# Two-layer encoder with three attention forms: the reciprocal roots of the projections' norms and the scale of the scores on GpSimd, lambda computed early in the stage

## Chip, cores and metric

The kernel runs on one core of a Trainium2 chip. The time is that of the whole program on the device, in microseconds (us); smaller is better. A profiled execution shows, for each engine, which instruction ran when: TensorE (PE, and PEld for its weight loads), VectorE (DVE), ScalarE (ACT), GpSimd (POOL) and SyncE (SP, which issues most DMAs).

## The reference, cut to what matters

Two layers over a sequence of 1024 tokens of 1024 features. Each layer normalises its input, projects it with one matrix, whose columns belong to three token mixers, and runs the mixers' attention; an output projection and a feed-forward part follow.

```
xn = _rms_norm(x, attn_norm[l])
h = xn @ w_in[l]
(h_cq, h_ckv, h_kr, h_dq, h_dk, h_dv, h_gq, h_gk, h_gv) = jnp.split(h, IN_OFFSETS, axis=-1)
c_q = _rms_norm(h_cq, mla_q_norm[l])
q_a = (c_q @ mla_w_uq[l]).reshape(B, S, MLA_HEADS, MLA_QK)...
c_kv = _rms_norm(h_ckv, mla_kv_norm[l])
kv_a = (c_kv @ mla_w_ukv[l])...
q_a, k_a = _rms_norm(q_a, mla_q_gain[l]), _rms_norm(k_a, mla_k_gain[l])    # then rotary
q_b = _apply_rope(_rms_norm(q_b, diff_q_gain[l]), cos_dif, sin_dif)
k_b = _apply_rope(_rms_norm(k_b, diff_k_gain[l]), cos_dif, sin_dif)
lam = exp(sum(diff_lq1[l] * diff_lk1[l])) - exp(sum(diff_lq2[l] * diff_lk2[l])) + lambda_init
a = p[:, :, 0] - lam * p[:, :, 1]                                          # differential attention
q_c = axial_rope(_rms_norm(q_c, gqa_q_gain[l]))
k_c = axial_rope(_rms_norm(k_c, gqa_k_gain[l]))
```

`_rms_norm(x, gain)` is x times the reciprocal root of the mean of its squares, times a gain. The softmax scale (width to the power -1/2) is folded into the norm of the queries.

## The kernel before, in words

**Stages of a layer.** The input's norm and the first projection; the other projections; attention (the three mixers' heads one behind the other); output projection and feed-forward. The projections run over groups of output columns: `down` for the two latents (`cq`, `ckv`), `diff_heads` for differential queries and keys in two groups each (`C_DQ`, `C_DK`), `mla_q` and `mla_kv` in two groups of three heads, `gqa_q`, `gqa_rest`, and the values (`diff_v`). Each runs over 8 tiles of 128 tokens. A product in full precision is three matmuls (L159, L160, L161) of high and low parts; the low part of a weight (`wl`, L125) is made on GpSimd here.

**From a tile's product to stored features.** ScalarE copies the sum from PSUM (`raw`), VectorE makes the two rotary products (L344, L349), GpSimd adds them into `half` (L411, L505; L497 multiplies by the gain where there is no rotation), ScalarE squares and VectorE sums the squares into `ssq` (L413, L509). `half` holds four tiles, 512 tokens; there are three such buffers. At each fourth tile `finish` (or the end of `down`) makes the reciprocal roots of all four: `rsq` forms `v` from `ssq` (L149), `newton` a first guess by integer operations (L132, L133) and three rounds of Newton's iteration, for 12 or 16 columns at once (4 in `down`). Then GpSimd multiplies `half` by the roots (L388), and `out_features` is put into the list `later`: TensorE transposes the four tiles (L364, into `pt`), ScalarE makes the high part (`sth`, L368), VectorE the low part (`stl`, L369; L373 with a gain), and SP stores both. In one layer's projections 22 norms go this way; two more, those of the input (`x_norm`), use `rsq` too.

**The rounds.** `newton` has two branches. Without an engine given, a round is three operations on VectorE (L136, L137, L138). With one it is four on that engine (L140 to L143). The norms of the attention's output pass `po` (GpSimd) already, in before too; the projections pass none.

**Lambda.** `neg_lambda` loads four vectors, multiplies two pairs of them on VectorE (L179), sums each product by a matmul with ones (L181, into `pl_`), takes the exponentials on ScalarE (L183) and combines them (L185, L186). In before its call stands at the end of the projections, behind the loop that empties `later`.

**What sets the order.** The context is opened with a scheduler that simulates a timeline (`schedule_with_timeline_sim=True`): each engine's queue is in the order that this simulation found, not in that of the code. Every engine then works through its queue in order and waits where an operand or a buffer isn't ready.

Of the kernel before, what the change touches and what calls it, by code (L numbers as in the profile page):

```python
# [16 lines left out]
ALU = mybir.AluOpType  # L17
# [48 lines left out]
def encoder(ctx: ExitStack, tc: tile.TileContext, a: dict, out: bass.AP):  # L66
    nc = tc.nc
    ve, ac, po, pe, sy = nc.vector, nc.scalar, nc.gpsimd, nc.tensor, nc.sync
# [29 lines left out]
    def ps_u(name):  # L98
        return banks["pool"].tile([P, 512], F32, tag="u", name=name)
# [11 lines left out]
    def f(t):  # L111
        return t.bitcast(F32)
# [14 lines left out]
    def newton(pool, v, n, tag, eng=None):  # L127

        i = pool.tile([P, n], I32, tag=tag + "i", name="i")
        t = pool.tile([P, n], F32, tag=tag + "t", name="t")  # L130
        r = pool.tile([P, n], F32, tag=tag + "r", name="r")
        ve.tensor_scalar(i, v.bitcast(I32), 1, None, ALU.arith_shift_right)  # L132
        ve.tensor_scalar(r.bitcast(I32), i, -1, 0x5F3759DF, ALU.mult, ALU.add)  # L133
        for _ in range(3):
            if eng is None:
                ve.scalar_tensor_tensor(out=t, in0=r, scalar=-0.5, in1=r, op0=ALU.mult, op1=ALU.mult)  # L136
                ve.tensor_tensor(out=t, in0=t, in1=v, op=ALU.mult)  # L137
                ve.scalar_tensor_tensor(out=r, in0=t, scalar=1.5, in1=r, op0=ALU.add, op1=ALU.mult)  # L138
            else:
                eng.tensor_tensor(out=t, in0=r, in1=r, op=ALU.mult)  # L140
                eng.tensor_tensor(out=t, in0=t, in1=v, op=ALU.mult)
                eng.tensor_scalar(t, t, -0.5, 1.5, ALU.mult, ALU.add)
                eng.tensor_tensor(out=r, in0=t, in1=r, op=ALU.mult)  # L143
        return r

    def rsq(pool, ssq, n, inv, scale, tag):

        v = pool.tile([P, n], F32, tag=tag + "v", name="v")
        ve.tensor_scalar(v, ssq, inv / scale**2, EPS / scale**2, ALU.mult, ALU.add)  # L149
        return newton(pool, v, n, tag)  # L150

    def gain_cols(src, n, name):
        t = lay.tile([P, n], F32, tag=name, name=name)
# [19 lines left out]
    def neg_lambda(l):  # L173
        lam_init = 0.8 - 0.6 * math.exp(-0.3 * l)
        lq = lay.tile([64, 4], F32, tag="lq", name="lq")
        for i, n in enumerate(("diff_lq1", "diff_lq2", "diff_lk1", "diff_lk2")):
            sy.dma_start(out=lq[:, i : i + 1], in_=a[n][l].unsqueeze(1))
        lp = lay.tile([64, 2], F32, tag="lp", name="lp")
        ve.tensor_mul(lp, lq[:, 0:2], lq[:, 2:4])  # L179
        pl_ = ps_u("pl_")  # L180
        pe.matmul(pl_[:, 0:2], ones[:64, :], lp, start=True, stop=True)  # L181
        le = lay.tile([P, 2], F32, tag="le", name="le")
        ac.activation(le, pl_[:, 0:2], AF.Exp)  # L183
        nlam = lay.tile([P, 1], F32, tag="nlam", name="nlam")
        ve.tensor_tensor(out=nlam, in0=le[:, 1:2], in1=le[:, 0:1], op=ALU.subtract)  # L185
        ve.tensor_scalar(nlam, nlam, -lam_init, None, ALU.add)  # L186
        return nlam
# [11 lines left out]
    for l in range(L):  # L199
# [15 lines left out]
        bp = tc.alloc_tile_pool(name=f"b{l}", bufs=2, side=there, reuse_waits="tile")  # L215
# [51 lines left out]
        def r_of(tt):  # L267
            return rx[tt // 4][:, tt % 4 : tt % 4 + 1]
# [24 lines left out]
        def run(*chunks):  # L293

            for _ in zip_longest(*chunks):
                pass
# [57 lines left out]
        def halves(n, nh):  # L354

            t = bp.tile([P, 4 * n], F32, tag="half", name="half", bufs=3, padded_shape=[P, 4 * 384])
            ssq = bp.tile([P, 4 * nh], F32, tag="ssq", name="ssq", bufs=3, padded_shape=[P, 16])
            return t.rearrange("p (t n) -> p t n", n=n), ssq.rearrange("p (t h) -> p t h", h=nh)

        def out_features(g, t, pieces, gains=None):  # L360
            for j, (c0, w, rows) in enumerate(pieces):
                pt = ps_u("pt")
                for i in range(4):
                    pe.transpose(pt[:w, i * P : (i + 1) * P], t[:, i, c0 : c0 + w], ident)  # L364
                h = bp.tile([P, 512], F32R, tag="sth", name="sth")[:w]
                lo = bp.tile([P, 512], F32R, tag="stl", name="stl")[:w]
                if gains is None:
                    ac.copy(h, pt[:w])  # L368
                    ve.tensor_tensor(out=lo, in0=pt[:w], in1=f(h), op=ALU.subtract)  # L369
                else:  # L370
                    gj = gains[:w, j : j + 1]
                    ac.activation(h, pt[:w], AF.Copy, scale=gj)
                    ve.scalar_tensor_tensor(  # L373
                        out=lo, in0=pt[:w], scalar=gj, in1=f(h), op0=ALU.mult, op1=ALU.subtract
                    )
                for part, st in ((0, h), (1, lo)):
                    sy.dma_start(out=rows[part][:, g * 512 : (g + 1) * 512], in_=f(st))

        def finish(g, t, ssq, nh, width, pieces, scaled):

            n = 4 * nh
            whole = width**-0.5 if scaled == nh else 1.0
            r = rsq(bp, ssq.rearrange("p t h -> p (t h)"), n, 1.0 / width, whole, "q")
            if 0 < scaled < nh:
                rv = r.rearrange("p (t h) -> p t h", h=nh)[:, :, :scaled]
                ve.tensor_scalar(rv, rv, float(width**-0.5), None, ALU.mult)
            tv = t.rearrange("p t (h x) -> p (t h) x", x=width)
            po.tensor_tensor(  # L388
                out=tv, in0=tv, in1=r.unsqueeze(2).to_broadcast([P, n, width]), op=ALU.mult
            )  # L390
            later.append([LAG, lambda: out_features(g, t, pieces)])
# [54 lines left out]
        def down(w, n, keep, gains, dst, extra):  # L446
            state = {}

            def emit(tt, ps):
                if tt % 4 == 0:  # L450
                    state["t"], state["ssq"] = halves(keep, 1)
                t, ssq = state["t"], state["ssq"].rearrange("p t h -> p (t h)")
                i = tt % 4
                ve.tensor_scalar_mul(t[:, i, :], ps[:, :keep], r_of(tt))
                if extra:
                    extra(tt, ps)
                ac.activation(work("sq", keep), t[:, i, :], AF.Square, accum_out=ssq[:, i : i + 1])
                if i == 3:
                    r = rsq(bp, ssq, 4, 1.0 / keep, 1.0, "q")
                    for j in range(4):  # L460
                        ve.tensor_scalar_mul(t[:, j, :], t[:, j, :], r[:, j : j + 1])
                    g = tt // 4
                    pieces = [(c0, P, [x[c0 : c0 + P] for x in dst]) for c0 in range(0, keep, P)]
                    later.append([LAG, lambda: out_features(g, t, pieces, gains)])

            return project(xn, KT, w, n, emit)

        def latent(src, nk):

            out = []  # L470
            for part in range(2):
                tiles = []
                for k in range(nk):
                    for th in range(2):
                        t = ops.tile([P, 512], F32R, tag="ab"[part], name="lat")
                        sy.dma_start(
                            out=f(t), in_=src[part, k * P : (k + 1) * P, th * 512 : (th + 1) * 512]
                        )
                        tiles.append(t)
                out.append(lambda k, tt, ts=tiles: ts[2 * k + tt // 4][:, tt % 4 * P : (tt % 4 + 1) * P])  # L480
            return out
# [72 lines left out]
        def diff_heads(col, c, gain, dst, scaled):  # L554
            pieces = [(j * P, P, rows_of(dst, 4 * c + 2 * j, 2)) for j in range(2)]
            t = tabs(gain, T_DIFF, DD, 32)
            return heads64(col + 256 * c, 4, 0, [(0, 4, t)], 32, pieces, 4 if scaled else 0)
# [16 lines left out]
        xpool.release()  # L574
        ops = tc.alloc_tile_pool(name=f"o{l}", bufs=10, side=here, reuse_waits="tile")
        run(diff_heads(C_DQ, 0, gd_q, qd, True))
        lat = latent(cqd, 3)
        tq = tabs(gq_m, T_MLA, ROPE, ROPE // 2)
        run(mla_q(0, tq))
# [12 lines left out]
        run(diff_v(1))  # L592
        for _, e in later:
            e()
        nlam = neg_lambda(l)
        bp.release()
        xnp.release()

# [32 lines left out]
        with tc.tile_pool(name=f"c{l}", bufs=2, side=there, reuse_waits="tile") as cp:  # L631
            QB = 256
            n = QB // P
# [91 lines left out]
            class Single:  # L725


                tag = "b"
# [31 lines left out]
            class Diff:  # L760
                tag = "a"
# [162 lines left out]
            while lagging or spreads or products or ends:  # L924
                done = front()
                whole = done is not False and not (fronts or twice[0])
# [280 lines left out]
        for ft in range(FT):  # L1207
# [3 lines left out]
            if ft % 2:  # L1211
# [3 lines left out]
                t = wr.tile([P, 2048], F32, tag="hs", name="hs", bufs=1)  # L1215
# [30 lines left out]
        for p0 in range(0, NP, NC):  # L1246
            n = min(NC, NP - p0)
# [102 lines left out]
```

## Time and profile before

| | us |
|---|---|
| median of three runs | 3217.32 |
| lowest and highest | 3216.38, 3220.18 |
| the profiled execution's own time | 3216.48 |
| its span in the profile | 3214.7 |

In the profiled execution TensorE is busy for 3080.5 us (96%), its weight loads for 84%, VectorE for 2317.8 us (72%), ScalarE for 1586.4 us (49%) and GpSimd for 1137.4 us (35%). A share over the span mixes stages with different limits, so the trace is read by stages. In layer 0 the projections behind the first one run from 86.6 to 373.4 us, and attention to 839.6; in layer 1 from 1684.2 to 1969.3, and attention to 2437.0. A row of the timeline names when an instruction began, how long it took, its engine, line and operands, and, in brackets, how long its engine had been idle before it and what it waited for.

### The profile page before, as it was taken

Reading aid. Unit: us, or ns where it says so; the run is one execution under the profiler, and the core shown is the slowest. Engines: PE = TensorE matmul, PEld = TensorE weight load, DVE = VectorE, ACT = ScalarE, POOL = GpSimd, SP = SyncE. Lnnn points to the kernel's source line nnn. Section 1 sums busy time; section 2 is a strip of 40 time slices with the busy share of each in tenths; the row PEclk is TensorE's granted clock in tenths of the full one; section 3 lists DMA queues with packets and bytes.
Section 4 is the critical chain, followed back from the end, with each engine's and each line's share of the span. In section 5 each row is a group of like instructions: output and inputs, shape, how many; then the busy total and the mean of one; then the engine's idle time right before and its main releaser. Section 6 shows DMA issues by size and latency. Waiting matters only on the chain.

```text
span 3214.7 us, 49930 instructions
## 1 busy us (share of the span) xinstructions
PE 3080.5 (96%) x17628; PEld 2697.1 (84%) x17628; DVE 2317.8 (72%) x4224; ACT 1586.4 (49%) x3010; POOL 1137.4 (35%) x1562
## 2 busy tenths in 40 slices
PE   8899899999998999989998998999999989999999
PEld 8899888888787888878898997888887878888787
DVE  5987788888347666677679877888882575665776
ACT  5444578877334333333254445878782443333332
POOL 1645477776102100100026454777771110111000
PEclk9999999999999999999999999999999999999999
DMA  5576633435652333473344756433356433335633
GB/s 155 160 215 196 197 114 106 120 101 156 201 187 76 104 112 99 137 248 128 98 157 144 230 181 184 126 101 111 103 154 223 157 95 99 101 106 168 223 123 102
DMA packets 386073, 466.14 MB, mean 145 GB/s; under 512 B 36768, under 2 KB 275360, under 8 KB 385824
## 3 DMA queue, kind: packets, MB, share of 16 engines
q1 hardware_dynamic: 372416, 418.38, 42.2%
q0 software_dynamic: 13408, 44.57, 4.2%
q8 instruction: 140, 2.29, 0.3%
q14 instruction: 109, 0.89, 0.1%
HBM read 313.42 MB, written 149.42 MB: 144 GB/s over the span
## 4 chain that ended last, share of the span: by engine, by line
PE 74%; DVE 12%; DMA 5%; ACT 3%; issue 3%; POOL 1%; SPq 1%; ACTq 0%; DVEq 0%; POOLq 0%
PE sc L681 8%; PE pv L890 8%; PE ptc L704 5%; PE psa L159 5%; PE psa L161 5%; PE psa L160 5%; PE psy L160 4%; PE psy L161 4%; PE psy L159 4%; PE psb L161 3%; PE psb L159 3%; PE psb L160 3%; PE psc L161 2%; PE psc L160 2%; PE psc L159 2%
## 5 line engine op out<-in xcount | busy, mean ns | idle before, releaser
L681 PE MATMUL sc<-k,q 128*128 128x512 f32 (+1 forms) x1472 | 417.7, 412 | 15.9 <-ACT p L689 9.0
L688 DVE TENSOR_REDUCE nm<-sc 128x1 f32<-128x1024 f32 x320 | 389.4, 1217 | 53.6 <-PE sc L681 50.6
L689 ACT ACTIVATE p<-sc,nm 128x1024 f32<-128x1024 f32 x320 | 358.7, 1121 | 66.2 <-DVE nm L688 51.7
L159 PE MATMUL psb<-wh,xl 128*128 128x256 f32 (+2 forms) x1280 | 381.1, 302 | 6.7 <-ACT wh L124 4.8
L160 PE MATMUL psb<-wl,xh 128*128 128x256 f32 (+2 forms) x1280 | 379.4, 298 | 7.7 <-POOL wl L125 7.5
L161 PE MATMUL psb<-wh,xh 128*128 128x256 f32 (+2 forms) x1280 | 377.4, 297 | 0.0
L710 DVE TENSOR_TENSOR pl<-ptc,ph 128x512 fp32r<-128x512 f32 x512 | 337.2, 680 | 34.6 <-ACT ph L709 33.0
L709 ACT CAST ph<-ptc 128x512 fp32r<-128x512 f32 x512 | 286.7, 586 | 75.7 <-PE ptc L704 65.4
L681 PEld LDWEIGHTS sc<-k,q 128*128 128x128 f32 (+1 forms) x1472 | 258.0, 190 | 66.7 <-ACT p L689 20.9
L704 PE MATMUL ptc<-ident,p 128*128 128x128 f32 x2048 | 289.7, 275 | 14.4 <-DVE pl L710 7.5
L890 PE MATMUL pv<-ph,v 128*128 128x256 f32 x1280 | 300.3, 287 | 0.0
L890 PE MATMUL pv<-pl,v 128*128 128x256 f32 x1024 | 277.7, 296 | 8.1 <-DVE ot L756 6.2
L704 PEld LDWEIGHTS ptc<-ident,p 128*128 128x128 f32 x2048 | 240.4, 142 | 47.1 <-POOL p L794 7.7
L1222 POOL DMA_DIRECT2D hd<-h x66 | 36.0, 545 | 680.5 <-DVE h L1163 434.8
L159 PE MATMUL psy<-bh,al 128*128 128x512 f32 x616 | 241.1, 394 | 14.7 <-DVE al L125 14.7
L160 PEld LDWEIGHTS psb<-wl,xh 128*128 128x128 f32 x1280 | 245.5, 192 | 10.6 <-POOL wl L125 10.1
L159 PEld LDWEIGHTS psb<-wh,xl 128*128 128x128 f32 x1280 | 244.9, 192 | 10.4 <-ACT wh L124 6.4
L744 POOL TENSOR_SCALAR p<-p,rec 128x1024 f32<-128x1024 f32 x192 | 215.0, 1123 | 107.5 <-DVE rec L694 84.7
L161 PEld LDWEIGHTS psb<-wh,xh 128*128 128x128 f32 x1280 | 245.1, 192 | 0.0
L160 PE MATMUL psy<-bl,ah 128*128 128x512 f32 x616 | 241.2, 392 | 0.1
L161 PE MATMUL psy<-bh,ah 128*128 128x512 f32 x616 | 240.5, 391 | 0.0
L124 ACT CAST wh<-ws 128x512 fp32r<-128x512 f32 x176 | 108.5, 622 | 266.9 <-PE psa L161 236.0
(222 smaller groups left out, 7654.6 us busy)
## 6 DMA issues: line engine op xcount, KB each, us to landing
graw<-in_w_gate_up SPq DMA_DIRECT2D x88, 512.0 KB, 5.5
ar<-hd SPq DMA_DIRECT2D x28, 1024.0 KB, 6.1
hd<-hs POOLq DMA_DIRECT2D x88, 256.0 KB, 3.1
hd<-h POOLq DMA_DIRECT2D x66, 256.0 KB, 2.4
q<-qd SPq DMA_DIRECT2D x256, 64.0 KB, 2.4
B<-od SPq DMA_DIRECT2D x12, 1280.0 KB, 6.8
wraw<-in_w_in SPq DMA_DIRECT2D x56, 256.0 KB, 3.5
o<-od SPq DMA_DIRECT2D x10, 1280.0 KB, 11.5
```

Of the source, the lines that this page charges most:

```text
L124: (hi_eng or ac.copy)(h, src)
L159: pe.matmul(ps, xl, wh, start=first, stop=False, skip_group_check=more)
L160: pe.matmul(ps, xh, wl, start=False, stop=False, skip_group_check=more)
L161: pe.matmul(ps, xh, wh, start=False, stop=last, skip_group_check=more)
L681: pe.matmul(ps[:, half, :], q[x][:, cut], kk[y], start=at == 0, stop=at == len(products) - 1)
L688: ve.tensor_reduce(nm, pf, axis=AX.X, op=ALU.max, negate=True)
L689: ac.activation(p, pf, AF.Exp, bias=nm, accum_out=s)
L704: pe.transpose(pt[:, k * P : (k + 1) * P], p[:, (4 * b + k) * P : (4 * b + k + 1) * P], ident)
L709: ac.copy(h, pv)
L710: ve.tensor_tensor(out=pl[:, 4 * b : 4 * b + 4, i * P : (i + 1) * P], in0=pv, in1=f(h), op=ALU.subtract,)
L744: po.tensor_scalar(p, p, r, 1.0, ALU.mult, ALU.mult)
L890: pe.matmul(b.o, x, y, start=first, stop=last)
```

## The change

`rsq` takes an engine and hands it to `newton`. `finish` and `down` give GpSimd, so the nine VectorE operations of their three rounds become twelve on GpSimd; `v` and the first guess stay on VectorE. The norm of the input (`x_norm`) keeps VectorE. The scale of a part of the queries (L386) becomes a GpSimd operation, with a second factor of 1. `neg_lambda` is called behind the first group of differential queries instead of at the end.

```diff
-    def rsq(pool, ssq, n, inv, scale, tag):
+    def rsq(pool, ssq, n, inv, scale, tag, eng=None):
 
         v = pool.tile([P, n], F32, tag=tag + "v", name="v")
         ve.tensor_scalar(v, ssq, inv / scale**2, EPS / scale**2, ALU.mult, ALU.add)
-        return newton(pool, v, n, tag)
+        return newton(pool, v, n, tag, eng)
...
             whole = width**-0.5 if scaled == nh else 1.0
-            r = rsq(bp, ssq.rearrange("p t h -> p (t h)"), n, 1.0 / width, whole, "q")
+            r = rsq(bp, ssq.rearrange("p t h -> p (t h)"), n, 1.0 / width, whole, "q", po)
             if 0 < scaled < nh:
                 rv = r.rearrange("p (t h) -> p t h", h=nh)[:, :, :scaled]
-                ve.tensor_scalar(rv, rv, float(width**-0.5), None, ALU.mult)
+                po.tensor_scalar(rv, rv, float(width**-0.5), 1.0, ALU.mult, ALU.mult)
...
                 if i == 3:
-                    r = rsq(bp, ssq, 4, 1.0 / keep, 1.0, "q")
+                    r = rsq(bp, ssq, 4, 1.0 / keep, 1.0, "q", po)
...
         run(diff_heads(C_DQ, 0, gd_q, qd, True))
+        nlam = neg_lambda(l)
         lat = latent(cqd, 3)
...
         for _, e in later:
             e()
-        nlam = neg_lambda(l)
         bp.release()
```

The scheduler finds another order for the whole program. Three places of layer 0 show it; in layer 1 they look alike.

GpSimd's queue, where the last `mla_q` group gets its roots (L388 with 1152 elements a row is the product with the roots of half an `mla_q` group; L551 belongs to the next projection). Before:

```order
L497 TENSOR_TENSOR half<-raw,mla_q_gain 128x3x64 x2
L388 TENSOR_TENSOR half<-half,r 128x1024
L505 TENSOR_TENSOR half<-half,tmp 128x3x32 x2
L125 TENSOR_TENSOR wl<-wraw,wh 128x2x256
L497 TENSOR_TENSOR half<-raw,mla_q_gain 128x3x64 x2
L388 TENSOR_TENSOR half<-half,r 128x1152
```

and in the changed kernel, up to the same L388:

```order
L388 TENSOR_TENSOR half<-half,r 128x1024
L141 TENSOR_TENSOR t<-t,v 128x12
L497 TENSOR_TENSOR half<-raw,mla_q_gain 128x3x64 x2
L505 TENSOR_TENSOR half<-half,tmp 128x3x32 x2
L142 TENSOR_SCALAR t<-t 128x12
L497 TENSOR_TENSOR half<-raw,mla_q_gain 128x3x64 x2
L143 TENSOR_TENSOR r<-t,r 128x12
L505 TENSOR_TENSOR half<-half,tmp 128x3x32 x2
L140 TENSOR_TENSOR t<-r 128x12
L141 TENSOR_TENSOR t<-t,v 128x12
L142 TENSOR_SCALAR t<-t 128x12
L143 TENSOR_TENSOR r<-t,r 128x12
```

The rounds stand between the other work of GpSimd, a step at a time where that work comes in between, and all twelve steps of a norm stand ahead of its L388. The two low parts of weights that stood here (L125) have moved ahead of these rows.

VectorE's queue where the last half of the last `mla_q` group is finished. Before, from its `v` to the low parts of the key group's transposes (`stl`):

```order
L149 TENSOR_SCALAR v<-ssq 128x12
L132 TENSOR_SCALAR i<-v 128x12
L133 TENSOR_SCALAR r<-i 128x12
L349 TENSOR_TENSOR tmp<-raw,tab 128x3x32
L136 SCALAR_TENSOR_TENSOR t<-r 128x12
L349 TENSOR_TENSOR tmp<-raw,tab 128x3x32
L137 TENSOR_TENSOR t<-t,v 128x12
L138 SCALAR_TENSOR_TENSOR r<-t,r 128x12
L336 TENSOR_TENSOR tab<-tab,gqa_q_gain 128x512
...
L454 TENSOR_SCALAR half<-psb,r 128x256 x2
L369 TENSOR_TENSOR stl<-pt,sth 128x512 x2
```

and in the changed kernel:

```order
L369 TENSOR_TENSOR stl<-pt,sth 128x512
L344 TENSOR_TENSOR krr<-krraw,tab 128x32
L349 TENSOR_TENSOR krtmp<-krraw,tab 128x32
...
L454 TENSOR_SCALAR half<-psb,r 128x256
L336 TENSOR_TENSOR tab<-tab,gqa_q_gain 128x512
L149 TENSOR_SCALAR v<-ssq 128x12
L336 TENSOR_TENSOR tab<-tab,gsw 128x512
```

The steps of the rounds are gone, and the key group's `stl` stands ahead of that `v` instead of behind it and its rounds.

TensorE's queue at the transposes of the second half of the first differential queries (`half_916` before, `half_925` in the changed kernel; numbers are the scheduler's). Before:

```order
L161 MATMUL psb_1320<-wh_1309,xh0_99 128x256
L159 MATMUL psb_1320<-wh_1315,xl0_100 128x256
L364 MATMUL pt_1389<-ident_63,half_916 128x128 x4
L364 MATMUL pt_1400<-ident_63,half_916 128x128 x4
L159 MATMUL psb_1411<-wh_1297,xl0_100 128x256
```

and in the changed kernel:

```order
L159 MATMUL psb_1564<-wh_1347,xl1_98 128x256
L160 MATMUL psb_1564<-wl_1348,xh1_97 128x256
L364 MATMUL pt_1421<-ident_63,half_925 128x128 x4
L364 MATMUL pt_1432<-ident_63,half_925 128x128 x4
L161 MATMUL psb_1564<-wh_1347,xh1_97 128x256
```

Before, they stand among the first tiles of the key group (`psb_1320`, first half of the tokens), behind 590 matmuls; now among its last (`psb_1564`, second half), behind 669. The transposes of the other norms of these four groups have moved back by 36 to 150 matmuls in the same way; the projections' own matmuls keep their order. The matmul of lambda (L181) now stands behind the transposes of the first half of these queries, ahead of the first `mla_q` group. The attention of layer 1 gets, on TensorE, VectorE, ScalarE and GpSimd, the order that the attention of layer 0 has in before; that of layer 0 a nearly unchanged one. The loads and the product L179 of lambda stand where they stood, near the start of the layer.

## Rows read from the trace of the kernel before

**Rows 1.** Busy time of each engine by stage, layer 0 and 1

```profile
core 0: us, PE busy (x) PEld busy (x) DVE busy (x) ACT busy (x) POOL busy (x), PEclk, DMA share, GB/s
...
86.60:164.40 77.80, 65.69 (x493) 63.04 (x492) 73.50 (x196) 32.53 (x84) 52.22 (x61) 0.96 0.48 151
164.40:373.40 209.00, 198.77 (x1488) 195.17 (x1486) 163.48 (x469) 87.83 (x230) 96.39 (x91) 0.99 0.67 205
373.40:839.60 466.20, 450.55 (x3008) 399.12 (x3008) 394.66 (x665) 367.93 (x728) 333.42 (x514) 0.99 0.41 120
...
1684.20:1761.90 77.70, 65.80 (x494) 63.48 (x494) 74.08 (x197) 32.80 (x85) 52.51 (x62) 0.96 0.48 148
...
1969.30:2437.00 467.70, 451.16 (x3008) 399.82 (x3008) 395.36 (x664) 367.92 (x730) 333.59 (x514) 0.99 0.42 119
```

**Rows 2.** Waits of TensorE, 86.6 to 164.4 us: total, times, longest

```profile
PE pt L364 <- DVE stl L369: 8.1, 4, 5.8
PE psb L160 <- POOL wl L125: 1.8, 1, 1.8
PE pt L364 <- POOL half L388: 1.6, 1, 1.6
```

**Rows 3.** Timeline ahead of TensorE's longest wait, several engines

```profile
153.44 2.12 POOL L388 TENSOR_TENSOR half<-half,r 128x1152 f32<-128x1152 f32 x1 [1.49 <-DVE r L138]
...
153.86 1.72 DVE L149 TENSOR_SCALAR v<-ssq 128x12 f32<-128x12 f32 x1
...
162.06 1.27 DVE L369 TENSOR_TENSOR stl<-pt,sth 128x512 fp32r<-128x512 f32 x2
...
162.88 1.92 PE L364 MATMUL pt<-ident,half 128*96 128x128 f32 x8 [5.76 <-DVE stl L369]
```

**Rows 4.** Busy times and granted clock around that wait, columns as in rows 1

```profile
160.00:170.00 10.00, 7.12 (x37) 7.09 (x38) 8.19 (x26) 4.89 (x23) 3.04 (x5) 0.66 0.61 197
```

**Rows 5.** VectorE's steps by line, 86.6 to 164.4 us: busy, mean ns | idle before

```profile
L136 DVE SCALAR_TENSOR_TENSOR t<-r 128x12 f32<-128x12 f32 (+1 forms) x21 | 7.7, 366 | 0.3
...
L137 DVE TENSOR_TENSOR t<-t,v 128x12 f32<-128x12 f32 (+1 forms) x21 | 6.2, 293 | 0.3
L138 DVE SCALAR_TENSOR_TENSOR r<-t,r 128x12 f32<-128x12 f32 (+1 forms) x21 | 5.6, 265 | 0.3
```

**Rows 6.** A step on GpSimd by shape, attention of layer 0

```profile
L141 POOL TENSOR_TENSOR t<-t,ov 128x2 f32<-128x2 f32 x48 | 9.8, 205 | 2.8
```

**Rows 7.** GpSimd's timeline there, first and last of seven steps in a row

```profile
412.81 0.19 POOL L140 TENSOR_TENSOR t<-r 128x2 f32<-128x2 f32 x1 [0.53 <-DVE r L133]
...
414.47 0.20 POOL L142 TENSOR_SCALAR t<-t 128x2 f32<-128x2 f32 x1
```

**Rows 8.** Timeline of a norm in the second part, several engines

```profile
199.87 0.17 DVE L136 SCALAR_TENSOR_TENSOR t<-r 128x16 f32<-128x16 f32 x1
...
201.22 0.74 POOL L411 TENSOR_TENSOR half<-half,tmp 128x256 f32<-128x256 f32 x1 [2.72 <-DVE tmp L349]
203.18 1.95 POOL L388 TENSOR_TENSOR half<-half,r 128x1024 f32<-128x1024 f32 x1 [1.22 <-DVE r L138]
...
205.19 0.98 PE L364 MATMUL pt<-ident,half 128*128 128x128 f32 x7
```

**Rows 9.** Waits of TensorE from 164.4 to 373.4 us

```profile
PE pt L364 <- POOL half L388: 1.9, 2, 1.5
```

**Rows 10.** Timeline at the first scores of both layers, TensorE and ScalarE

```profile
373.40 1.22 PE L681 MATMUL sc<-k,q 128*128 128x512 f32 x2 [3.39 <-ACT le L183]
...
1968.72 1.28 ACT L183 ACT_TABLE_LOAD   x1
...
1969.28 2.30 PE L681 MATMUL sc<-k,q 128*128 128x512 f32 x7 [2.92 <-DVE vst L431]
```

**Rows 11.** Timeline of GpSimd and VectorE at 118 us

```profile
118.00 2.84 POOL L388 TENSOR_TENSOR half<-half,r 128x1152 f32<-128x1152 f32 x1 [1.05 <-DVE r L138]
...
118.11 0.41 DVE L344 TENSOR_TENSOR half<-raw,tab 128x256 f32<-128x256 f32 x1
```

## Prediction

> **What bounds the kernel now.** I read first the busy time of each engine by stage. In the attention stages TensorE is busy for 450.55 of 466.20 us [rows 1]: nothing that the change touches could bring much there. The stretch from 86.6 to 164.4 us of layer 0 (the first two differential query and key groups and the two latent query groups, `mla_q`) is another matter: TensorE is busy for 65.69 of 77.80 us, and VectorE for 73.50, that is 94.5% [rows 1]. It has a twin in layer 1 of 77.70 us [rows 1]. GpSimd is busy for 52.22 of them, 67%. The rest of the projections, 164.4 to 373.4, has TensorE at 198.77 of 209.00 and VectorE at 163.48 [rows 1]: little is to be had there.
>
> Then the waits of TensorE in that stretch: 8.1 us for `stl` of L369 on VectorE (four times, the longest 5.8), 1.8 for a weight's low part (`wl`) and 1.6 for L388, both on GpSimd [rows 2]; together 11.5 of the 12.1 us in which it is not busy. The longest is at 162.88: eight transposes wait 5.76 us for `stl`, which VectorE begins only at 162.06 [rows 3]. What made VectorE late is seen by its queue: L149, an operation of 12 columns, takes 1.72 us at 153.86, under a GpSimd L388 that began at 153.44 and took 2.12 [rows 3]; behind it stand the seed, nine steps and the table products, and L369 behind those. After the wait TensorE's granted clock is lower: 0.66 over 160 to 170 us, so part of it at 1.2 instead of 2.4 GHz [rows 4]. Ahead of this fall it had stood still for 5.76 us.
>
> **The change part by part.** *Steps off VectorE.* In the stretch 63 operations of L136 to L138 go, those of seven norms: 7.7, 6.2 and 5.6 us, in all 19.5 [rows 5]. An undisturbed one takes 0.17 [rows 8], so 63 x 0.17 = 10.7 of this is work, and 8.8 is waiting for something else, as L149's was. What is left on VectorE is 73.5 - 19.5 = 54.0 us, or 62.8 if the 8.8 of waiting passes on to whatever stands there next. Either way VectorE stops being the fullest engine of the stretch.
>
> *Steps onto GpSimd.* The other branch of `newton` has four operations to a round, so 84 come. Before has no step of 12 or 16 columns on GpSimd, but 192 of 2 columns: 0.205 us for L141 in layer 0's attention [rows 6]. The time does not lie in the columns there, so I take 0.20. Seven in a row start from 412.81 to 414.47, one every 0.277 [rows 7]: that is the upper bound, for steps of one chain with nothing between them; the lower one is VectorE's 0.17, as no row shows GpSimd quicker. 84 x 0.20 = 16.8 (14.3 to 23.3), so GpSimd goes from 52.2 to 69.0 us (66.5 to 75.5). I take the middle because the new order mixes the chains with other work of GpSimd. It becomes the fullest engine.
>
> What the stretch then lasts I take from the share that the fullest engine reaches now: 94.5%. 69.0 / 0.945 = 73.0 instead of 77.8: **-4.8 us in each layer**. The floor is TensorE's 65.7. It isn't reached by this reckoning, since a chain of twelve steps on GpSimd stands in one queue with L388, L411, L497, L505 and the weights' low parts, and each of them waits for what is ahead. Every group of transposes of these seven norms now stands 36 to 150 matmuls later on TensorE, so the chains have room; but there are three buffers of `half`, and the last `mla_q` half can't be written before the key group's transposes have read theirs.
>
> *The second part, 164.4 to 373.4.* VectorE isn't full there, so only lengthened chains count. At 199.87 the first step of a norm begins, at 203.18 L388, and the transposes start at 205.19, as L388 ends (203.18 + 1.95 = 205.13) [rows 8]: no slack. From 199.87 to 203.18 are 3.3 us. On GpSimd twelve steps in a row are 12 x 0.277 = 3.3, and one L411 of 0.74, which stands between them, makes 4.0: +0.7. TensorE's waits for L388 in this stretch are two, 1.9 us in all [rows 9]; the other places have slack of some us, and I add 0.1. **+0.8 in each layer**, from 0 up to 3 x 1.8 = 5.4 if at all three places the chain is longer by the full difference of 12 x 0.277 and nine at 0.17.
>
> *The scale of the scores* (L386) is one small operation, twice in each layer. It stands in a chain of the second part; 0.27 against 0.17 is inside the 0.1. **0**, and 0.2 if uncovered.
>
> *Lambda.* Its loads and its first product were early in the old order already; what moves are a matmul of two columns, the two exponentials and two small operations. Layer 1's first score is held by `vst` of the last projection (2.92 us), layer 0's by `le`, whose own wait is behind the same `vst` [rows 10]: without `le` the store of that projection is next. **0**, from -0.1 to +0.4. Its load of ScalarE's table moves into the stretch, where ScalarE is busy for 32.53 of 77.80 us [rows 1]; uncovered it is 1.3 us in layer 1, the only one that has such a load there [rows 10].
>
> *Attention.* Its order in layer 1 becomes, instruction by instruction, that which layer 0 has before, and layer 0 takes 466.20 where layer 1 takes 467.70 [rows 1]: **-1.5**. Layer 0's new order is close to the old one; 0, give or take 1.5.
>
> The sum: 2 x (-4.8) + 2 x 0.8 - 1.5 = -9.5 us. The profiled execution took 3216.48, 0.8 below the median of the runs; 3216.48 - 9.5 = **3207.0 us**.
>
> **A rule that speaks against it.** L149's 1.72 us under L388 [rows 3] say that some VectorE operations stand still while GpSimd reads. Against that, at 118.00 an L388 and an L344 run side by side: L344 takes 0.41 us for 256 columns, and L388 2.84 [rows 11] instead of 2.12. So the exclusion is not whole. The Trainium skill (SBUF — State Buffer, "Who interferes with whom") says that the two engines share a pair of ports, which one of them holds for a whole instruction, when VectorE reads two operands from SBUF or works in a two-port mode. By that rule, work moved from one to the other frees nothing, and L149 agrees with it where L344 does not. The sum goes by the rows of busy time; the fourth rival is what the exclusion alone would make.
>
> **The rivals.** *All waits go.* If the new order gives every chain enough room, TensorE keeps none of the 11.5 us [rows 2], nor the slow clock behind them: 7.12 us busy at 0.66 [rows 4] lose about 2. That is -13.5 + 0.8 in each layer, -1.5 once: 3189.6 us. For it: the transposes stand far later. Against it: a GpSimd at 69.0 us of work in 66 would be over full.
>
> *Nothing comes of it.* The waits only change place: VectorE's 8.8 us of waiting pass on to L344, L349 and L369, and TensorE waits for L388 at the key group's transposes in place of `stl`. The stretch stays at 77.8, and the second part's +1.6 and attention's -1.5 cancel: 3216.6. For it: the waits on GpSimd (1.8 and 1.6 us) are already there [rows 2].
>
> *Slower: GpSimd becomes the bound.* At 0.277 each the steps make 75.5 us of work, and 75.5 / 0.945 = 79.9: +2.1; with half of the second part's bound, 2.7, it is +4.8 in each layer, -1.5 once: 3224.6. The point from which the stretch is longer than before is (73.5 - 52.2) / 84 = 0.254 us for a step. For it: the only run of steps in a row [rows 7]; against it: the order has other work between them.
>
> *Slower: the exclusion.* If each step on GpSimd holds off VectorE for as long as it lasts, the two together lose 10.7 us of work and gain 16.8: +6.1 in each layer, with the second part 6.9, -1.5 once: 3228.8. It decides from 10.7 / 84 = 0.127 us for a step. For it: L149 [rows 3]; against it: L344 [rows 11], and steps that are short.
>
> **How the numbers follow.** A measurement of this kernel can tell some 0.2%, 6.4 us, from no change. The forecast has a chance of 0.34 (its own range 3201 to 3211), all waits gone 0.16, nothing 0.28, GpSimd's pace 0.12, the exclusion 0.10. So faster by over 0.2% 0.34 + 0.16 = 0.50, within 0.28, slower 0.12 + 0.10 = 0.22. The range reaches from just below the case in which all waits go to the exclusion's: 3188 to 3229; outside remain the tails of the two, about 0.15.
>
> **What would show it.** In the stretch of the changed kernel: VectorE near 54 us if the waiting goes with the steps, near 63 if it passes on; GpSimd at 67 to 75; steps of 12 and 16 columns at 0.17 to 0.28; `stl` no longer the first row of TensorE's waits, nor a wait of 5 us; the granted clock above the 0.96 of [rows 1]. The wrong sign would show as TensorE's waits for L388 or `wl` above 8 us, or as L388 starting later than now at the places of the second part; a step that takes 0.254 us or more decides against the stretch. Layer 1's attention should last 466.2 us. If the two stretches last as before with VectorE at 54, the bound was a chain and not the fullest engine, and the step that failed is the 94.5%.

## The result and the profile after

The changed kernel takes 3198.28 us, median of four runs (3195.51 to 3199.07), against 3216.85 for the kernel before, measured with it: a ratio of 0.9939, with a 95% interval of 0.9922 to 0.9957. So it is 0.4 to 0.8% faster. The forecast was 3207.0 with a range of 3188 to 3229: the time lies in the range, on the side that was forecast, and the gain is nearly twice the forecast one. The profiled run of the changed kernel took 3195.51 us, with a span of 3193.7, which is 21.0 less than that of before.

The stretch of [rows 1] can't be cut out at the same clock times any more. I use marks that both kernels have on TensorE: the first matmul of `mla_q` (86.39 us in before), the first of `gqa_q` (181.03), and the first score of attention (373.40). Between the first two lies what I call the first part, then the second part. The busy times between the marks, both layers, of before (columns as in [rows 1]):

```profile
86.39:181.03 94.64, 82.53 (x611) 79.88 (x610) 85.07 (x233) 41.79 (x117) 56.84 (x69) 0.95 0.50 155
181.03:373.40 192.37, 182.14 (x1373) 178.54 (x1371) 152.13 (x432) 78.77 (x196) 91.98 (x84) 1.00 0.67 208
...
1684.05:1778.41 94.36, 82.46 (x611) 80.13 (x609) 85.45 (x233) 41.63 (x117) 56.69 (x69) 0.95 0.50 152
1778.41:1969.28 190.87, 180.32 (x1374) 177.07 (x1372) 152.68 (x432) 79.09 (x196) 91.81 (x84) 1.00 0.67 209
```

and of the changed kernel:

```profile
85.96:172.31 86.35, 78.63 (x601) 76.45 (x601) 64.39 (x159) 39.45 (x114) 74.23 (x163) 0.98 0.49 156
172.31:359.19 186.88, 181.59 (x1378) 180.45 (x1377) 128.79 (x316) 81.13 (x197) 129.07 (x243) 0.99 0.70 218
...
1673.85:1760.32 86.47, 78.72 (x601) 76.65 (x601) 65.35 (x158) 41.02 (x115) 73.31 (x163) 0.98 0.49 156
1760.32:1949.90 189.58, 181.21 (x1378) 179.02 (x1376) 130.31 (x317) 81.20 (x199) 129.55 (x243) 0.99 0.70 217
```

The first part is shorter by 8.3 and 7.9 us, the second by 5.5 and 1.3. The border between them moves: eight transposes of the last norms have passed over it (72 instead of 80 lie in layer 0's first part). Behind it the changed kernel has a wait of 2.4 us for L461 that before has not, and TensorE's granted clock is 0.63 over the 4.6 us that follow this wait, so a part of them at 1.2 instead of 2.4 GHz. A part of what the first part gains is lost again there. With the border at the first matmul of `gqa_rest` (206.04 us in before), the part ahead of it is shorter by 3.5 and 2.5 us, and the part from there to the first score by 10.3 and 6.7. VectorE falls from 85.07 to 64.39 us in the first part, GpSimd rises from 56.84 to 74.23. The share of the fullest engine beside TensorE falls from 90% (85.07 of 94.64) to 86% (74.23 of 86.35). The granted clock rises from 0.95 to 0.98.

The waits of TensorE in layer 0's first part, changed kernel (wait, total, times, longest), to be compared with [rows 2]:

```profile
PE pt L364 <- POOL half L388: 4.4, 2, 3.5
PE pt L364 <- DVE stl L369: 2.2, 3, 1.6
PE psb L159 <- ACT raw L492: 1.1, 2, 0.8
```

`stl` is no longer the first row, and its longest wait is 1.6 instead of 5.8 us. L388 has taken its place, with one wait of 3.5. What L388 was behind shows in the timelines of VectorE, GpSimd and TensorE there:

```profile
144.24 1.90 POOL L388 TENSOR_TENSOR half<-half,r 128x1024 f32<-128x1024 f32 x1
...
146.18 1.22 DVE L133 TENSOR_SCALAR r<-i 128x12 int32<-128x12 int32 x1 [4.49 <-POOL half L388]
...
149.07 1.90 POOL L388 TENSOR_TENSOR half<-half,r 128x1024 f32<-128x1024 f32 x1
...
151.02 1.29 PE L364 MATMUL pt<-ident,half 128*128 128x128 f32 x8 [3.46 <-POOL half L388]
```

VectorE stands still for 4.49 us until the L388 of 144.24 has ended. L133 writes a tile of roots, of which there are two, and that L388 reads the tile written two norms earlier. The eight transposes at 151.02 are those of the key group's second half. By the trace they have moved back by only 24 of the projections' matmuls (383 to 407, counted from the first of `mla_q`), less than the 36 that were taken as the least.

The steps themselves, changed kernel, first part of layer 0 (lines, busy and mean):

```profile
L140 POOL TENSOR_TENSOR t<-r 128x12 f32<-128x12 f32 (+2 forms) x24 | 6.3, 267 | 2.7 <-DVE r L133 2.7
L141 POOL TENSOR_TENSOR t<-t,v 128x12 f32<-128x12 f32 (+2 forms) x24 | 5.5, 237 | 0.3
L142 POOL TENSOR_SCALAR t<-t 128x12 f32<-128x12 f32 (+2 forms) x24 | 5.3, 229 | 0.2
L143 POOL TENSOR_TENSOR r<-t,r 128x12 f32<-128x12 f32 (+2 forms) x24 | 5.2, 223 | 0.2
```

These are 96 steps of eight norms in 22.3 us, 0.232 each.

### The profile page after: what moved, and what is told of

The parts are those of the page before. It is cut to its first block, busy times and chain, and to the rows that moved or that the text cites. A ratio compares the mean times of both kernels' runs of the same rounds, so it can differ in the third digit from the quotient of the medians.

```text
span 3193.7 us, 50051 instructions
## 1 busy us (share of the span) xinstructions
PE 3074.3 (96%) x17628; PEld 2694.2 (84%) x17628; DVE 2220.0 (70%) x3788; ACT 1589.2 (50%) x3010; POOL 1262.2 (40%) x2142
## 4 chain that ended last, share of the span: by engine, by line
PE 55%; issue 20%; DVE 9%; DMA 6%; POOL 5%; ACT 3%; SPq 1%; POOLq 0%; ACTq 0%; DVEq 0%
PE sc L681 8%; PE pv L890 8%; PE ptc L704 5%; PE psa L159 3%; PE psa L160 3%; PE psa L161 3%; PE psb L160 2%; PE psb L161 2%; PE psb L159 2%; PE psd L159 2%; PE psd L160 2%; PE psd L161 2%; PE psy L160 2%; PE psy L161 2%; PE psy L159 2%
## 5 line engine op out<-in xcount | busy, mean ns | idle before, releaser
L124 ACT CAST wh<-ws 128x512 fp32r<-128x512 f32 x176 | 108.4, 622 | 268.0 <-PE psa L161 237.5
```

Source lines behind the costliest of these rows:

```text
L124: (hi_eng or ac.copy)(h, src)
```

## The experiments

e1 to e12 were each timed in five rounds against the kernel before, on the same chip (e5 to e8 on another one than the rest); `before` is its median there. The ratio compares the runs of both, with a 95% interval.

| kernel | median us | before | ratio | interval |
|---|---|---|---|---|
| the change | 3198.28 | 3216.85 | 0.9939 | 0.9922 to 0.9957 |
| e1 steps only | 3197.78 | 3218.04 | 0.9938 | 0.9925 to 0.9950 |
| e2 lambda only | 3213.63 | 3218.04 | 0.9988 | 0.9979 to 0.9997 |
| e3 all transposes later | 3230.10 | 3218.04 | 1.0038 | 1.0024 to 1.0052 |
| e4 `down` on VectorE | 3191.56 | 3218.04 | 0.9923 | 0.9909 to 0.9937 |
| e5 `finish`'s transposes later | 3214.10 | 3215.04 | 0.9998 | 0.9990 to 1.0007 |
| e6 steps in the first four groups | 3202.05 | 3215.04 | 0.9963 | 0.9950 to 0.9975 |
| e7 a fourth round | 3199.72 | 3215.04 | 0.9944 | 0.9931 to 0.9958 |
| e8 two rounds on VectorE | 3202.00 | 3215.04 | 0.9959 | 0.9947 to 0.9972 |
| e9 four buffers | 3192.30 | 3215.72 | 0.9930 | 0.9917 to 0.9943 |
| e10 four buffers, `down` on VectorE | 3191.59 | 3215.72 | 0.9931 | 0.9915 to 0.9947 |
| e11 before, four buffers | 3216.11 | 3215.72 | 1.0005 | 0.9996 to 1.0014 |
| e12 steps in the second part | 3207.25 | 3215.94 | 0.9970 | 0.9958 to 0.9982 |

### Steps alone, lambda alone

e1 is the changed kernel with L386 on VectorE and `neg_lambda` at its old place. e2 moves only `neg_lambda`:

```diff
         run(diff_heads(C_DQ, 0, gd_q, qd, True))
+        nlam = neg_lambda(l)
...
             e()
-        nlam = neg_lambda(l)
```

> The Newton steps of finish and down on GpSimd as in the changed kernel; the scale (L386) on VectorE and lambda at the end, as before. Theory (the steps are what counts): the part from the first latent matmul to the first matmul of gqa_q lasts 86 to 87 us in each layer, as in the changed kernel (86.35 and 86.47; before 94.64 and 94.36), and the time is 3200 to 3203, that is the changed kernel's 3198.3 plus at most the 2 to 5 us that the ends of the two projection stages have gained. Rival (lambda and the scale carry a good part): above 3207, half of the 18.6 gone.

> Only the call of neg_lambda moved; steps and scale on VectorE as before. The order of the projections on TensorE stays that of before but for its matmul. Theory (lambda is worth next to nothing, as I predicted): 3216 to 3217, the stretch still 94.5 us, the first score of layer 0 waiting for the last vst instead of le by about as long as the 3.39 us now. Rival (le at the end was the wait): the 3.39 us of layer 0 go or fall below 1 us, 3212 to 3214.

e1 has the whole gain: 0.9938. So the rival falls that lambda and the scale carry a good part of it. e2 by itself is faster by 0.03 to 0.21%, about 4 us, more than the nothing that I forecast, though both kinds of call cost the same beside the moved steps: 0.9938 without lambda, 0.9939 with it. In e2's profile the first score of layer 0 has no wait for `le`, but its first part (94.51 us) and second part (192.05) are those of before. Where its 4 us lie in the runs I can't show from that one execution, which at 3216.44 is one of its slower ones.

### Is it the order?

The change moves VectorE's work, and in consequence the transposes. e3 puts all transposes off with the steps still on VectorE; e5 only those of `finish`.

```diff
-        LAG = 6000
+        LAG = 9000
```
```diff
-            later.append([LAG, lambda: out_features(g, t, pieces)])
+            later.append([LAG + 3000, lambda: out_features(g, t, pieces)])
```

> The kernel before with the transposes of out_features put off by half as much again (LAG 9000 instead of 6000); all steps on VectorE, lambda at the end. Theory (VectorE's load is the bound of the stretch): VectorE still has 85 us of work in the part that lasts 94.5, so the part stays above 91 us and the time between 3210 and 3220. Rival (the gain of the change came from its transposes standing later, not from the other engine): the part falls to 86 to 88 us and the time to 3198 to 3204.

> The kernel before with the transposes of finish put off by half as much again, those of down (the latents) as before; all steps on VectorE, lambda at the end. In e3, where the latents' transposes were late too, the part from the first latent matmul to gqa_q lost 7.7 and 5.3 us to waits for the latents themselves; without these it would have been 88.3 and 88.0 us. Theory (VectorE's load is the bound): the part stays above 91 us, the time 3212 to 3220. Rival (later transposes alone do most of it): the part is 86 to 89 us in each layer, 6 to 8 less than before, and the time 3202 to 3208.

e3 is slower by 0.4%: TensorE waits 6.4 us for the first latent, whose transposes were put off too, so the experiment didn't tell what it was made for. e5 tells more. Its first part, and then the waits of TensorE in its second part from `gqa_rest` on:

```profile
84.26:173.42 89.16, 81.96 (x610) 80.13 (x609) 81.50 (x230) 40.70 (x115) 58.13 (x69) 0.94 0.47 150
```
```profile
PE psb L159 <- ACT wh L124: 3.9, 4, 1.3
PE pl__5137 L181 <- DVE stl L369: 2.9, 1, 2.9
PE sc L681 <- DVE stl L369: 2.4, 1, 2.4
PE pt L364 <- DVE stl L369: 2.2, 3, 1.0
```

The first part does fall, by 5.5 us in layer 0 and 3.7 in layer 1. So part of its length was indeed the place of the transposes. But VectorE has as much to do as before, and it is late elsewhere: in the second part it makes TensorE wait 2.9 and 2.4 us at the end of the stage, and the time doesn't change (0.9998). This order alone only carries the wait along. It isn't the order of the changed kernel, though: e5 puts off the transposes of the second part too, and 20 of them stand behind the last matmul of the projections. What the changed kernel's own order would bring without the moved steps no run shows. That the load counts by itself is shown by e8 (next section): its transposes stand on TensorE within some 20 matmuls of their places in before.

### How much by which steps

e8 keeps the steps on VectorE and leaves out the third round, so the roots are less exact. e7 adds a fourth round on GpSimd.

```diff
-        for _ in range(3):
+        for _ in range(2 if tag == "q" else 3):
```
```diff
-        for _ in range(3):
+        for _ in range(4 if tag == "q" else 3):
```

> The kernel before with two rounds instead of three in the projections' norms, all on VectorE: a third of the steps is left out, 21 operations or 6.5 us of VectorE's time in the stretch. Theory (the load of VectorE ahead of stl is the bound): about a third of the gain of the stretch, 2 to 4 us in each layer, 3209 to 3214. Rival (the steps matter only as places where VectorE stands still behind GpSimd, which moves on to other instructions): 0 to 1 us, 3215 to 3219.

> The changed kernel with a fourth round of Newton's iteration in the projections' norms, 28 more steps on GpSimd in the stretch, 88 in a layer's projections; the roots stay the same within rounding. As my forecast had it (GpSimd as the fullest engine sets the length of the stretch): 28 x 0.245 / 0.86 = 8 us more in each layer, 3212 to 3216. Rival (the steps hide in gaps of GpSimd, and chains and buffers bound the stretch): 0 to 2 us in each layer, 3198 to 3202.

A third less of the steps on VectorE gives 0.41%, two thirds of what the whole change gives. 72 operations go in each layer (by the trace 24 norms of a layer's projections take these steps, not 22), and 13 us in all: each is worth 0.09 us, where an undisturbed one takes 0.17. On GpSimd a third more costs nothing that can be measured: 0.9944 against 0.9939. From the first matmul of `mla_q` to the first of `gqa_rest`, both layers, e7 has

```profile
86.80:203.37 116.57, 107.08 (x809) 104.83 (x809) 89.28 (x211) 53.75 (x143) 101.12 (x237) 0.96 0.54 173
1677.15:1792.04 114.89, 103.78 (x810) 101.67 (x810) 91.59 (x211) 54.97 (x144) 101.35 (x237) 0.99 0.56 178
```

and the changed kernel

```profile
85.96:202.09 116.13, 106.00 (x817) 103.50 (x817) 84.55 (x212) 53.70 (x145) 94.57 (x200) 0.97 0.58 184
1673.85:1789.97 116.12, 105.84 (x817) 103.56 (x817) 85.53 (x211) 55.21 (x146) 93.71 (x200) 0.97 0.58 185
```

GpSimd has 6.6 and 7.6 us more to do there, and the lengths are nearly the same: +0.4 and -1.2 us. My forecast's rule, length = GpSimd's work / 0.945, would have made 7 to 8 us more in each layer. Up to `gqa_q` alone e7 is longer than the changed kernel (90.45 and 87.63 us against 86.35 and 86.47), but it has made up for that at `gqa_rest`, and its time isn't longer.

### Which part of the projections

e6 gives GpSimd's steps to `finish` only up to the last `mla_q` group, e12 only from `gqa_q` on; `down` stays on VectorE in both (e6's expectation counts norms of `down`, wrongly). `finish` passes `steps[0]` to `rsq`. In e6:

```diff
+        steps = [po]
         run(down(w_cq, QR, QR, g_cq, cqd, None))
...
         run(mla_q(1, tq))
+        steps[0] = None
```

> The steps on GpSimd only from the first latent to the last mla_q group of each layer, seven norms of 12 or 16 columns and the four of the first latent's and differential queries' neighbours that lie there; VectorE from the second latent on. Lambda and scale as before. Theory (the gain is made in that stretch): 3198 to 3202, the part from the first latent matmul to gqa_q 85 to 87 us. Rival (a good part of the gain is made behind it): 3204 to 3210.

> The complement of e6: finish's steps on GpSimd only from gqa_q on, on VectorE in the first four groups and in down; lambda and scale as before. TensorE's order is that of before up to gqa_q, so the stretch with its waits of 5.5 us for stl must stay at 94 to 95 us. As my forecast had the second part (only chains get longer there): 0 to 1.6 us slower, 3216 to 3219. Theory after e6 and e1 (0.9963 and 0.9938): VectorE's steps delay TensorE in the second part as well, and moving them there brings the missing 0.25%, 3206 to 3210. Rival (the difference of e6 and e1 comes from down's norms, or only together with a relieved stretch): 3213 to 3217.

They add up: 0.9963 and 0.9970 make 0.9933. The nearest kernel with all of `finish`'s steps moved and `down`'s not is e4 with 0.9923, and e1, with `down`'s too, has 0.9938; with intervals of about 0.0013 to either side these agree. The steps of the first four groups bring 12 us (0.37% of 3215), 5.9 in each layer; those of the second part bring 9.6, 4.8 in each layer, where I had forecast a loss of 0.8. These are shares by the steps that were moved. Where the time is gained is another matter, by the profiles (one execution each, layer 0 and 1, us):

| kernel | first `mla_q` to `gqa_rest` | `gqa_rest` to first score |
|---|---|---|
| before | 119.65, 118.64 | 167.36, 166.59 |
| the change | 116.13, 116.12 | 157.10, 159.93 |
| e6 | 116.98, 115.38 | 162.08, 162.83 |
| e12 | 119.20, 117.67 | 164.45, 162.94 |

In e6, all of whose moved steps lie ahead of `gqa_q`, 5.3 and 3.8 us are gained behind `gqa_rest`, more than the 2.7 and 3.3 ahead of it. So a relief of VectorE in one group also shows in later groups. Why, these runs don't show. (e11, with TensorE waiting as in before, has 120.64 and 118.89, 166.52 and 165.88: two executions can differ by about 1 us here.)

In e12's layer 0 the first part lasts 94.90 us and keeps its wait of 5.65 for `stl`. TensorE's waits in the second part of before, from 181.03 to 373.4, beside that of [rows 9]:

```profile
PE psb L159 <- ACT wh L124: 2.6, 2, 1.9
...
PE psb L160 <- POOL wl L125: 1.3, 2, 1.1
PE psb L159 <- DVE vst L125: 0.8, 2, 0.5
```

and in e12, from 181 to 372:

```profile
PE pt L364 <- POOL half L388: 3.7, 3, 2.1
PE sc L683 <- ACT le L183: 1.2, 1, 1.2
PE psb L160 <- POOL wl L125: 0.6, 2, 0.4
PE psb L159 <- ACT wh L124: 0.4, 1, 0.4
```

The wait for L388 does grow, 1.9 to 3.7 us: the chains are longer on GpSimd, as forecast. But the others fall by 3.7, from 2.6 + 1.3 + 0.8 to 0.6 + 0.4, and the wait ahead of the first score from 3.39 to 1.2. This last one is the largest. `le` stands on ScalarE behind the last `vst`, which waits for the store of an earlier `vst`, and these stores stand in SP's queue behind those of `sth` and `stl`. Layer 0 of before, the last `stl` and that `vst`:

```profile
367.66 0.69 DVE L369 TENSOR_TENSOR stl<-pt,sth 128x512 fp32r<-128x512 f32 x1 [1.33 <-DMA km<-stl]
```
```profile
372.82 0.47 ACT L430 ACTIVATE vst<-psb,r 128x256 fp32r<-128x256 f32 x1 [3.31 <-DMA vd<-vst]
```

and in e12:

```profile
362.06 0.69 DVE L369 TENSOR_TENSOR stl<-pt,sth 128x512 fp32r<-128x512 f32 x1 [0.26 <-ACT sth L368]
```
```profile
367.95 0.47 ACT L430 ACTIVATE vst<-psb,r 128x256 fp32r<-128x256 f32 x1 [3.25 <-DMA vd<-vst]
```

The two traces have to be compared from a common mark, the first matmul of `gqa_q` (181.03 and 179.78). From there the `stl` begins 4.4 us earlier in e12, and both that `vst` and the first score (373.40 and 368.53) 3.6 us earlier, which is the whole gain of layer 0's second part (192.37 to 188.75 us). The weights `wh` for which TensorE waits 1.9 us in before come only 0.4 us earlier by that count (L124 at 312.51 and 310.83); for the rest, that wait is shorter because TensorE comes later. That the earlier `stl` causes the earlier `vst` is read from the order in SP's queue; no run holds a store back by itself.

### `down`'s norms and the buffers of the roots

e4 gives `down` its old call of `rsq` in the changed kernel; e9 gives the four small tiles of a norm four buffers instead of two; e10 has both; e11 has e9's edit in the kernel before.

```diff
-                    r = rsq(bp, ssq, 4, 1.0 / keep, 1.0, "q", po)
+                    r = rsq(bp, ssq, 4, 1.0 / keep, 1.0, "q")
```
```diff
+    def more(tag):
+        return dict(bufs=4) if tag == "q" else {}
...
-        r = pool.tile([P, n], F32, tag=tag + "r", name="r")
+        r = pool.tile([P, n], F32, tag=tag + "r", name="r", **more(tag))
```

> The changed kernel with down's norms back on VectorE, finish's on GpSimd. In the changed kernel TensorE waits 2.40 and 2.53 us for L461, the product with the roots of down's last norm. Theory (that chain of twelve steps in GpSimd's queue is what is late): both waits fall below 1 us and the time is 3194 to 3196. Rival (the wait only passes on to the next norm or buffer): within 1.5 us of 3198.3.

> The changed kernel with four buffers instead of two for the small tiles of rsq and newton (v, i, t, r) in the projections. In the changed kernel VectorE stands still for 4.49 us at 146.18, ahead of L133, which writes a root's tile that an earlier norm's L388 on GpSimd has still to read; TensorE then waits 3.46 for L388. Theory (with the steps on GpSimd this reuse of two buffers is the next wait): the 4.49 goes, the waits of 3.46 and 3.48 at the key group's transposes fall below 2 us, 3192 to 3196. Rival (GpSimd's queue is what is late there, the buffer only stands in the same place): within 2 us of the changed kernel's 3198, the wait for L388 as long as before.

> The kernel of e4 (finish's steps on GpSimd, down's on VectorE, lambda early) with four buffers as in e9. If both edits help on their own, 3186 to 3190; if only one of the two does, 3190 to 3194; if neither, 3195 to 3199.

> The kernel before with four buffers as in e9. With all steps on VectorE a root's tile is read by L388 long before the norm after the next begins; TensorE's order is unchanged. Expected: no change, 3213 to 3219, its part from the first latent matmul to gqa_q 94 to 95 us. If the buffers matter here too, below 3211, and e9's gain, if any, is not the change's own new wait.

e4's mechanism fell: the waits for L461 are 5.06 and 2.44 us, not below 1, though the kernel is as fast as any. So these waits aren't made by the twelve steps on GpSimd. VectorE's queue ahead of the longer one shows other delays:

```profile
179.86 0.69 DVE L369 TENSOR_TENSOR stl<-pt,sth 96x512 fp32r<-96x512 f32 x1 [3.56 <-DMA qm<-stl]
180.46 1.64 DVE L136 SCALAR_TENSOR_TENSOR t<-r 128x4 f32<-128x4 f32 x1
...
185.79 1.75 DVE L136 SCALAR_TENSOR_TENSOR t<-r 128x4 f32<-128x4 f32 x1
...
189.53 1.12 DVE L461 TENSOR_SCALAR half<-half,r 128x256 f32<-128x256 f32 x4
```

It waits 3.56 us for the store of an earlier `stl`, and two steps take 1.64 and 1.75 us beside an L125 of GpSimd (at 180.24 and 185.21). How much of the 5.06 us each of these makes was not tested.

In e9, TensorE's waits in layer 0's first part (lines are three higher there) are:

```profile
PE psb L162 <- ACT raw L495: 2.5, 3, 1.9
PE pt L367 <- DVE stl L372: 1.9, 1, 1.9
PE psb L162 <- ACT krraw L551: 0.4, 1, 0.4
```

The 3.5 us for L388 is gone, and VectorE's 4.49 us with it. The first part is 85.59 us against 86.35 in layer 0 and 87.66 against 86.47 in layer 1, so the wait was there, but hardly on the path. VectorE's queue in e9 tells why:

```profile
147.32 0.49 DVE L347 TENSOR_TENSOR half<-raw,tab 128x96 f32<-128x96 f32 x2 [5.38 <-PE pt L367]
```

At the same place it now stands still for 5.38 us, until transposes have read a buffer of `half`, and this product begins at 147.32 us where it began at 147.33 in the changed kernel (as L344). By this row the three buffers of `half` were the next limit there. e11 shows that four buffers of the roots did nothing in the kernel before. e10, with both edits, is no faster than either alone. e4, e9 and e10 have the lowest medians, 3191.6 to 3192.3; their intervals overlap that of the change, and none was timed directly against it.

## Why the prediction was right, and where not

**The bound.** That VectorE's load in the projections sets TensorE's waits was right: e8 takes steps from VectorE without giving them to anyone, nearly keeps the order, and has two thirds of the gain. e5 leaves VectorE's load, moves the order, and has none of it; but its order is not that of the change.

**The steps' price.** 0.20 us was taken, inside 0.17 to 0.277. It is 0.232 for 4 to 16 columns.

**The waiting behind GpSimd.** Of the two cases, 54 and 62.8 us left on VectorE, the first came: with the marks used here, L136 to L138 had 8.2 + 6.6 + 6.1 = 20.9 us in the first part, and VectorE fell by 85.07 - 64.39 = 20.7. Three `stl` and one L454, 2.7 us, have crossed the border, so for the same work it is some 18 of the 20.9: most of the 8.8 us of waiting went with the steps. So the rival of exclusion falls, too: with 0.232 for a step, far above its point of 0.127, it forecast a loss. The prediction took from the Trainium skill's rule of the shared ports (SBUF — State Buffer, "Who interferes with whom") that moved work frees nothing; this fall doesn't agree with that. The section itself speaks of instructions that overlap in time. Single pairs may still hold each other up here: L149 took 1.72 us under an L388 [rows 3], and L133 above 1.22 us at 146.18, beside an L125 of GpSimd from 146.10.

**The length of the first part, -4.8 us in each layer.** The steps of these groups bring 5.9 by e6, so the size was near, but by luck: the way to it was wrong, and part of that time is gained behind the stretch. The length isn't GpSimd's work divided by 0.945: e7 gave GpSimd 7 us more to do, and up to `gqa_rest` it took as long. The fullest engine of before was the bound because TensorE's transposes waited for its results (8.1 us for `stl`, [rows 2]), not because it was the fullest; GpSimd's chains have room, since the transposes stand later. The rival of GpSimd's pace falls by e7. The rival that all waits go didn't come either: 7.7 us of them are left in layer 0's first part.

**The second part, +0.8.** This is the step that failed. "VectorE isn't full there, so only lengthened chains count" overlooked that an engine busy for 79% (152.13 of 192.37 us) still delays single results: e12 shows -0.30%, 4.8 us gained in each layer. In layer 0 TensorE's waits for L388 did grow by 1.8 us, about twice the 0.8 that I had set for the chains; the other waits fell by more.

**Lambda and the scale, 0.** Beside the moved steps right (e1 against the change); lambda alone is worth 0.03 to 0.21%. L386 takes 0.232 us on GpSimd.

**Attention, -1.5 in layer 1.** From the first score to the first matmul of the output projection layer 1 took 468.61 us before and 466.79 in the changed kernel, but layer 0 took 467.14 and 468.31. In the other kernels' profiles the same stage varies from 465 to 473; so a term of this size can't be read from one execution.

The sum was half of what came, a gain of 9.5 us against 18.6. The second part is enough to make the difference: its steps bring 9.6 us where I had put a loss of 1.6. The range held because it reached from the rival in which all waits go to that of the exclusion.

## What to carry to other kernels

An engine need not be full to be what others wait for: ask which of its results are late, and on whose queue, even where it is busy for only four fifths of the time. Before a rule from busy shares is used for a forecast, a variant that adds to the supposed new bound (here a fourth round on GpSimd) says in a single run whether it is one. And delaying the waiting work instead of relieving the late engine moves a wait to the next place: e5's first part was 5.5 us shorter, and its time the same.

## What the runs showed of the hardware

In the first part small steps of 4 to 16 columns took 0.232 us on GpSimd, where L141 with 2 columns took 0.205 [rows 6]; a third more of them (e7) cost no time that could be measured. VectorE's same steps took 0.17 undisturbed [rows 8] and 0.27 to 0.37 on average in the loaded stretch of before [rows 5]. Most of that surplus went with them, though GpSimd was busy for 17 us longer there.
